# Half of an attention output projection in seven block products, with the operand sums on VectorE

## The chip, the cores and the metric

The kernel runs on one core of a Trainium2 chip. The core has five engines that run side by side, each with its own instruction queue: TensorE (PE, matrix products; its weight loads are listed as PEld), VectorE (DVE), ScalarE (ACT), GpSimd (POOL) and SyncE (SP, which only starts transfers here). The metric is the device time in microseconds of one execution. Two kernels are compared by the median of several executions.

## The reference

A two-layer encoder is run over two sequences, of 512 and 256 tokens, with shared weights. Each layer adds half a gated feed-forward block, a token mixer and another half feed-forward block to the residual stream x. The mixer of the second layer is windowed attention with 16 query heads of 64 channels and 4 key heads. What matters here is its last line:

```python
o = jnp.einsum('bnhgqk,bnkhd->bnqhgd', (p / denom).astype(v.dtype), vband)
return o.reshape(B, T, Hq * d) @ w_o        # (tokens x 1024) times (1024 x 1024)
...
x = x + mix
x = x + 0.5 * swiglu_ffn(rmsnorm(x, norm_g[li, 2]), ffn_w1[li, 1], ffn_w2[li, 1])
```

So each of the 768 tokens' 1024 attention outputs is multiplied with w_o and added to x, then x is normalised and goes into the last feed-forward block, which is called f3.

## The kernel before

**Numbers.** Everything is float32. An operand of a product is split into a high part (rounded to the format that TensorE takes in one pass) and the rest: ScalarE copies the high part, VectorE subtracts (`split`, lines 391 to 393). A product is then three matmuls: high by high, high by low, low by high (`mm3`, lines 385 to 389).

**Memory.** Activations lie in 21 slots of 128 x 1536 floats (`big`, line 91). Raw weights come from memory in tiles of 128 x 1024 (`wr`, four buffers), started on SP's queue, and their split halves go into eight buffers (`w`). A plan lists all weights in the order of their use; `load_next` starts the loads of the next entry when raw buffers are free, and `done` (line 365) frees the buffers of a used weight and stages as many next ones as fit. An accumulating transfer, started on POOL's queue, adds one tile to another in memory (`into`, line 159). A framework under the kernel works out all semaphores and lays down the order of each engine's queue ahead of the run; an instruction can be put ahead of one that stands earlier in the program if its operands are expected earlier.

**Products in blocks.** The feed-forward blocks already multiply 2 x 2 blocks (the two halves of tokens, of the channels summed over, and of the output columns) with seven products instead of eight, at the price of sums of the operands and of the results. `plan_quad` and `quad_steps` (line 209) load and add up the weights for it: p1 to p6 use the raw tiles or sums of them, p7 uses a third sum, s3. `down_last` (line 800) runs the products in the order LAST = p1, p2, p6, p7, p4, p5, p3. FACTOR (line 39) says which activation factor each product takes: b00, b10, b11 are plain blocks, t1 to t4 are sums.

**The attention stage.** `swa` (line 1428) works through 24 units: 4 key heads (groups) times 6 blocks of 128 tokens. `pipeline` (line 1585) interleaves the steps of the units, four steps a unit, and `extra` puts other work at given steps: the query projection, reloading x, splitting attention outputs, and pieces of the output projection. A unit's `finish` (line 1701) writes its outputs into `of[g]`, for the first 21 units by transfers, for the last three by ScalarE and VectorE directly. `of[g]` holds 256 channels of all 768 tokens, so groups 0 and 1 give the first half of the 1024 input channels of w_o, and groups 2 and 3 the second half.

**The output projection** (`out_proj`, line 1514) runs twice. Its first half (groups 0 and 1) is woven into the pipeline from step 66 on. Its second half (groups 2 and 3) follows the pipeline: for each of two column halves and six token blocks, four channel blocks of three matmuls with 512 columns each, then VectorE adds the bank to x (`add_x`, line 846). The outputs of groups 2 and 3 are split by `split_out` (line 1490) in pieces of 512 and 256 columns, those of group 2 from step 83 on, those of group 3 behind the pipeline. In the second column half, each block of x that is complete is normalised by `after_block` (line 590): ScalarE squares and sums it, VectorE scales it. When three blocks are normalised, `turn` (line 470) transposes them on TensorE, ScalarE copies them out and splits them with VectorE into f3's operands (b00 and b10 for the first half of tokens, b01 and b11 for the second). `run_later` starts such deferred steps. f3 opens with `up_first` (line 650): plain products on the first half of tokens, then the products p7 and p3 of a seven-product pair.

Of the kernel before, what the change touches and what calls it, by code (L numbers as in the profile page):

```python
# [9 lines left out]
F32 = mybir.dt.float32  # L10
F32R = mybir.dt.float32r
# [5 lines left out]
P = 128  # L17
D = 1024
DFF = 2816
NC = D // P  # L20
# [14 lines left out]
H = T // 2  # L35
HB = H // P
# [16 lines left out]
LAST = ("p1", "p2", "p6", "p7", "p4", "p5", "p3")  # L53
TAIL = (("b00", "b10"), ("t3", "t2"), ("t4", "t1"), ("b11",))
FACTOR = {"p1": "b00", "p2": "b10", "p3": "b11", "p4": "t4", "p5": "t1", "p6": "t2", "p7": "t3"}
# [3 lines left out]
class Trunk:  # L59
# [149 lines left out]
    def quad_steps(self, key, raws, srcs, order):  # L209
        nc = self.nc  # L210
        flat = lambda t: t.rearrange("p a b -> p (a b)")
        up = len(raws) == 2
        if up:
            a11, a12, a21, a22 = (flat(t[:, h : h + 4, :]) for t in raws for h in (0, 4))
            part = lambda i, k: srcs[i].rearrange("(k p) c -> p k c", p=P)[:, k : k + 4, :]
# [5 lines left out]
        if not up:  # L221
            self.into(a21, a22)
        s3 = []
        for i, src in enumerate(three):
            t = self.wp.tile([P, 512], F32, tag="s3", name=self.name("s3"), bufs=2)
            self.last_load = nc.sync.dma_start(t.rearrange("p (a b) -> p a b", a=src.shape[1]), src)
            self.into(t, a11 if up else a11[:, i * 512 : (i + 1) * 512])
            s3.append(t)
# [21 lines left out]
        add = {"second": lambda: nc.vector.tensor_add(a11, a11, a21), "fourth": lambda: nc.vector.tensor_add(a12, a12, a11)}  # L250
# [3 lines left out]
        if order == OPEN:  # L254
            own.update({"p3": s3[1:], "p7": s3[:1]})
            add = {"second": lambda: self.into(a11, a21)}
            behind, pin = {"p1": "second"}, lambda ins: None
        elif order == DOWN:
            before = {}
            add = {"second": lambda: self.into(a11, a21), "fourth": lambda: self.into(a12, a11)}  # L260
# [938 lines left out]
        quad(("g",), w_in[:, 2 * D : 3 * D], TOK)  # L1199
        quad(("o",), w_o, OUT)  # L1200

    def plan_out(self, tag, w_o):
        for half in range(2):
            for c in range(2):
                for i in range(2):
                    lo = half * 512 + i * 256
                    self.plan((tag, half, c, i), w_o[lo : lo + 256, c * 512 : (c + 1) * 512], (2, 512))

    def plan_swa(self, w_qkv, w_o):
        for tag, c in (("kv", D), ("q0", 0), ("q1", 512)):  # L1210
            self.plan_tok(tag, w_qkv, c)
        self.plan_out("sw_o", w_o)

    def hgrn(self, lb_row, gn_row, next_row):
        nc = self.nc
# [212 lines left out]
    def swa(self, next_row):  # L1428
        nc = self.nc
# [32 lines left out]
        def put_q(half):  # L1462
            def f(s, b, ps):
                gb = SEQS[s][0] // P + b
                if half and gb % 3 == 0:
                    hold.append(self.big([P, 3, 512]))
                t = hold[gb // 3][:, gb % 3] if half else self.xt()[:, :512]
                self.rotate(ps, 512 // HD, b, t)
                for gg in range(2):
                    qtok[(s, b, half * 2 + gg)] = t[:, gg * 256 : (gg + 1) * 256]  # L1470

            hold = []
            return f

        tiles = [None] * NC
        of = {}

        def units(gs):
            def alloc(g):
# [10 lines left out]
        def split_out(g, i, s):  # L1490
            off, n = SEQS[s]
            if s == 0:
                tiles[2 * g + i] = self.big([P, 2, T], F32R)
            hi, lo = (tiles[2 * g + i][:, half, off : off + n] for half in range(2))
            self.split(of[g][:, i, off : off + n], hi, lo)

        q = itertools.chain(self.proj_tok("q0", put_q(0)), self.proj_tok("q1", put_q(1)))
        wo = self.out_proj("sw_o", 0, tiles, None)
        for _ in range(8):
            next(q)  # L1500
        piece = lambda g: lambda: next(g, None)
        extra = [(i * 5 / 4 - 4, piece(q)) for i in range(16)]
        extra += [(18 + 2 * i, piece(q)) for i in range(25)]
        extra.append((46, self.reload_x))
        for n in range(12):
            extra.append(((50, 58, 83)[n // 4] + 2 * (n % 4), lambda n=n: split_out(n // 4, n // 2 % 2, n % 2)))
        extra += [(66 + i * 3 / 2, piece(wo)) for i in range(24)]
        self.pipeline(list(units(range(KV))), extra)
        for n in range(4):
            split_out(3, n // 2, n % 2)  # L1510
        self.drain(wo)
        self.drain(self.out_proj("sw_o", 1, tiles, next_row))

    def out_proj(self, tag, half, act, next_row):
        for c in range(2):
            for b in range(NBLK):
                ps = self.ps()
                sl = slice(b * P, (b + 1) * P)
                for i in range(4):
                    key = (tag, half, c, i // 2)  # L1520
                    wh, wl = self.take(key)
                    t = act[half * 4 + i]
                    self.mm3(ps, (t[:, 0, sl], t[:, 1, sl]), (wh[:, i % 2, :], wl[:, i % 2, :]), i == 0, i == 3)
                    if i == 1:
                        if b == NBLK - 1:
                            self.done(key)
                        yield
                self.add_x(self.x[b][:, c * 512 : (c + 1) * 512], ps, 1.0)
                if b == NBLK - 1:
                    self.done(key)  # L1530
                if half and c:
                    self.after_block(b, next_row)
                    if b in (HB - 1, HB):
                        self.run_later()
                elif not half and b % 2:
                    self.run_later()
                yield

# [293 lines left out]
```

## Time and profile before

| what | us |
|---|---|
| median of 3 executions (2751.13 to 2752.06) | 2751.23 |
| the profiled execution, its own time | 2750.38 |
| its span, from the first to the last instruction | 2748.6 |
| second half of the output projection, in the trace | about 2222 to 2257.4 |

The granted TensorE clock was 0.999 of full speed. The profile comes from one execution. Its page gives the busy time of each engine, the chain of work that ended last (followed back from the last instruction to whatever released it), and the costliest groups of instructions. The trace behind it can be asked for a stretch of time: the busy time of each engine in windows, or the instructions of one engine in order of time. A row of the latter shows start, duration, engine, line of the kernel, operation, output and inputs, and in brackets how long the engine had idled before and what ended the wait. In a row of windows come the stretch and its length, then for PE, PEld, DVE, ACT and POOL the busy time and the number of instructions, then the granted clock, the DMA share and GB/s.

### The profile page before, as it was taken

What the parts mean: (1) busy time and instruction counts of PE and PEld (TensorE: products, weight loads), DVE (VectorE), ACT (ScalarE), POOL (GpSimd) and SP (SyncE); (2) the same over time, 40 slices, a digit from 0 to 9 for tenths busy, and PEclk for the clock granted to TensorE, in tenths of its full rate; (3) what the DMA queues carried; (4) which work ended last, traced back from release to release, by engine and by line L of the source; (5) the groups of instructions that cost most, each with busy time, mean ns of one, the idle gap of its engine ahead of it and who ended that gap; (6) DMA issues with size and microseconds to landing.
All of it is one profiled execution on the core that took longest, in us unless ns stands there. A gap on an engine that the chain in (4) does not pass through costs nothing.

```text
span 2748.6 us, 41245 instructions
## 1 busy us (share of the span) xinstructions
PE 2733.9 (99%) x15059; PEld 2541.0 (92%) x15059; DVE 2164.3 (79%) x3759; ACT 1405.6 (51%) x2665; POOL 500.4 (18%) x566
## 2 busy tenths in 40 slices
PE   9999999999999999999999999999999999999998
PEld 8999999989999889999998999999888889999997
DVE  8788788767877889787878977787847869787877
ACT  6344444634454676444455643444458856444444
POOL 1111121200000111211121121111005621211120
PEclk9999999999999999999999999999999999999999
DMA  6665556741122756556555655555424436555553
GB/s 180 141 143 143 134 136 165 228 140 39 39 59 65 200 131 154 140 142 146 137 129 138 142 142 142 143 139 128 134 75 112 88 76 147 138 145 144 138 127 111
DMA packets 367867, 357.49 MB, mean 130 GB/s; under 512 B 15832, under 2 KB 276400, under 8 KB 367664
## 3 DMA queue, kind: packets, MB, share of 16 engines
q1 hardware_dynamic: 307200, 227.18, 27.8%
q0 software_dynamic: 56160, 114.19, 23.2%
q10 hardware_dynamic: 4304, 13.49, 1.4%
q8 instruction: 118, 1.93, 0.3%
q14 instruction: 85, 0.70, 0.1%
HBM read 228.45 MB, written 15.73 MB: 89 GB/s over the span
## 4 chain that ended last, share of the span: by engine, by line
PE 96%; DVE 2%; ACT 1%; DMA 0%; issue 0%; POOL 0%; ACTq 0%; SPq 0%; DVEq 0%; POOLq 0%
PE ps L678 44%; PE ps L787 17%; PE ps L1003 6%; PE ps L820 6%; PE ps L389 5%; PE ps L388 5%; PE ps L387 5%; PE ps L1066 3%; PE ps L1171 1%; PE ps L484 1%; PE ps L1686 1%; PE ps L1147 1%; PE ps L1698 0%; PE ps L1648 0%; PE ps L1699 0%; PE ps L1649 0%
## 5 line engine op out<-in xcount | busy, mean ns | idle before, releaser
L678 PE MATMUL ps<-big,w 128*128 128x384 f32 x6972 | 1213.2, 334 | 0.0
L678 PEld LDWEIGHTS ps<-big,w 128*128 128x128 f32 x6972 | 1209.5, 188 | 1.4
L243 ACT CAST w<-wr 128x512 fp32r<-128x512 f32 (+1 forms) x615 | 428.6, 706 | 671.8 <-PE ps L678 349.2
L244 DVE TENSOR_TENSOR w<-wr,w 128x512 fp32r<-128x512 f32 (+1 forms) x541 | 437.7, 813 | 141.9 <-ACT w L243 107.7
L787 PE MATMUL ps<-w,big 128*128 128x512 f32 x2016 | 460.9, 390 | 0.0
L787 PEld LDWEIGHTS ps<-w,big 128*128 128x128 f32 x2016 | 376.7, 188 | 80.1 <-ACT big L392 1.5
L850 DVE SCALAR_TENSOR_TENSOR x<-ps,x 128x512 f32<-128x512 f32 x420 | 274.6, 682 | 26.5 <-PE ps L787 13.5
L160 POOL DMA_DIRECT2D s<-wr x135 | 119.6, 935 | 887.4 <-issue 283.6
L160 POOL DMA_DIRECT2D wr<-wr x147 | 129.0, 877 | 796.3 <-DVE big L393 149.9
L393 DVE TENSOR_TENSOR big<-tA,big 128x384 fp32r<-128x384 f32 x308 | 179.2, 593 | 21.1 <-ACT big L392 20.9
L392 ACT CAST big<-tA 128x384 fp32r<-128x384 f32 x308 | 152.6, 514 | 74.1 <-DVE tA L712 29.2
L387 PE MATMUL ps<-big,w 128*128 128x384 f32 x544 | 187.3, 345 | 0.6 <-DVE big L464 0.6
L388 PE MATMUL ps<-big,w 128*128 128x384 f32 x544 | 183.2, 337 | 0.2 <-DVE big L464 0.2
L389 PE MATMUL ps<-big,w 128*128 128x384 f32 x544 | 182.6, 336 | 0.3 <-DVE w L393 0.3
L1003 PE MATMUL ps<-w,big 128*128 128x512 f32 x756 | 178.2, 393 | 0.1
L820 PE MATMUL ps<-w,big 128*128 128x512 f32 x756 | 174.7, 391 | 0.7 <-DVE x L850 0.6
L820 PEld LDWEIGHTS ps<-w,big 128*128 128x128 f32 x756 | 141.1, 188 | 30.8 <-DVE x L850 1.9
L1003 PEld LDWEIGHTS ps<-w,big 128*128 128x128 f32 x756 | 140.3, 188 | 29.0 <-DVE w L393 0.6
L244 POOL TENSOR_TENSOR w<-wr,w 128x512 fp32r<-128x512 f32 x74 | 105.3, 1424 | 122.1 <-ACT w L243 121.4
L393 DVE TENSOR_TENSOR w<-wr,w 128x1024 fp32r<-128x1024 f32 (+1 forms) x74 | 87.8, 1193 | 30.6 <-ACT w L392 28.6
L392 ACT CAST w<-wr 128x1024 fp32r<-128x1024 f32 (+1 forms) x74 | 75.7, 1029 | 69.7 <-PE ps L388 36.0
L706 DVE TENSOR_TENSOR tA<-tA,ps 128x384 f32<-128x384 f32 x80 | 44.0, 550 | 81.4 <-PE ps L678 81.4
(251 smaller groups left out, 3730.0 us busy)
## 6 DMA issues: line engine op xcount, KB each, us to landing
wr<-in_ffn_w_dram SPq DMA_DIRECT2D x254, 512.0 KB, 3.8
s<-wr POOLq DMA_DIRECT2D x135, 256.0 KB, 4.5
s<-in_ffn_w_dram SPq DMA_DIRECT2D x126, 256.0 KB, 3.2
wr<-wr POOLq DMA_DIRECT2D x61, 512.0 KB, 5.5
wr<-wr POOLq DMA_DIRECT2D x86, 256.0 KB, 3.7
wr<-in_hg_w_in_dram SPq DMA_DIRECT2D x32, 512.0 KB, 3.8
spill<-x ACTq DMA_DIRECT2D x12, 512.0 KB, 3.8
kept<-big POOLq DMA_DIRECT2D x8, 768.0 KB, 6.1
```

The costliest lines, as they stand in the source:

```text
L160: self.nc.gpsimd.dma_start(out, src, accum_op=ALU.add)
L243: nc.scalar.copy(h, src)
L244: (eng or nc.vector).tensor_sub(l, src, h.bitcast(F32))
L387: nc.tensor.matmul(out, a[0], b[0], start=first, stop=False)
L388: nc.tensor.matmul(out, a[0], b[1], start=False, stop=False)
L389: nc.tensor.matmul(out, a[1], b[0], start=False, stop=last)
L393: self.last_lo = self.nc.vector.tensor_sub(lo, src, hi.bitcast(F32)).ins
L678: self.nc.tensor.matmul(ps, a[x], b[y], start=first and k == 0 and i == 0, stop=k == 3 and i == 2, skip_group_check=True,)
L787: nc.tensor.matmul(ps, a[x], w[y], start=name == chain and kp == 0 and q == 0, stop=kp == 1 and q == 2, skip_group_check=True,)
L820: nc.tensor.matmul(ps, a[x], w[y], start=name == chain and k == 0 and q == 0, stop=k == 2 and q == 2, skip_group_check=True,)
L850: self.nc.vector.scalar_tensor_tensor(x, ps, c, x, ALU.mult, ALU.add)
L1003: nc.tensor.matmul(ps, x[:, sl], y, start=fresh and k == 0 and q == 0, stop=k == 3 and q == 2, skip_group_check=True,)
```

## The change

The second half of the output projection becomes a 2 x 2 block product with seven products in the order LAST. The token halves are 384 tokens (three blocks), the channel halves are groups 2 and 3, the column halves 512 columns. Its weights are planned as one entry of four raw tiles with `plan_quad`; the third sum of weights takes its two tiles from the activation slots instead of the buffers `s3`, which the attention units use. The splitting of groups 2 and 3 by 128-channel tiles is replaced by seven factors of 384 tokens: b00 and the first subtraction (`lead`) at steps 83 and 86, b10 behind the pipeline, and the others as hooks between the blocks of p1 and p6. The sums t2, t3, t4 are made and split on VectorE and ScalarE in two parts: `early` (256 of the 384 tokens) and `late` (the last 128). `out_quad` adds the results to x: p1 is copied out by ScalarE; p6 and p7 are combined with it on VectorE and also added to a second block of x by accumulating transfers on POOL's queue (`into`); the others are added or subtracted by VectorE. The first token half of x is complete after p4, the second after p3.

```diff
@@ quad_steps
         s3 = []
+        more = self.big([P, 2, 512]) if key[0] == "sw_o" else None
         for i, src in enumerate(three):
-            t = self.wp.tile([P, 512], F32, tag="s3", name=self.name("s3"), bufs=2)
+            t = more[:, i] if more else self.wp.tile([P, 512], F32, tag="s3", name=self.name("s3"), bufs=2)
...
@@ plan_swa (plan_out is taken out)
-        self.plan_out("sw_o", w_o)
+        for c in range(2):
+            for i in range(2):
+                self.plan(("sw_o", 0, c, i), w_o[i * 256 : (i + 1) * 256, c * 512 : (c + 1) * 512], (2, 512))
+        rows = w_o[512:, :].rearrange("(h k p) c -> h p k c", p=P, k=2)
+        srcs = [rows[h][:, :, c * 512 : (c + 1) * 512] for c in range(2) for h in range(2)]
+        self.plan_quad(("sw_o", 1), srcs, (2, 512), LAST)
...
@@ swa
+        whole, early, late = slice(0, H), slice(0, 2 * P), slice(2 * P, H)
+        part = lambda g, half, at=whole: of[g][:, :, half * H + at.start : half * H + at.stop]
+
+        def factor(name, src, at=whole):
+            if name not in facs:
+                facs[name] = self.big([P, 2, 2, H], F32R)
+            self.split(src, *(facs[name][:, :, i, at] for i in range(2)))
+
+        def lead():
+            nc.vector.tensor_sub(part(2, 0), part(2, 0), part(2, 1))
+
+        def mixed(at):
+            add, sub = nc.vector.tensor_add, nc.vector.tensor_sub
+            b11 = part(3, 1, at)
+            for name, op, out, x, y in (
+                ("t2", add, part(2, 0, at), part(2, 0, at), b11),
+                ("t3", sub, part(2, 1, at), part(2, 1, at), b11),
+                ("t4", sub, part(3, 0, at), part(3, 0, at), part(2, 0, at)),
+            ):
+                op(out, x, y)
+                factor(name, out, at)
...
-        for n in range(12):
-            extra.append(((50, 58, 83)[n // 4] + 2 * (n % 4), lambda n=n: split_out(n // 4, n // 2 % 2, n % 2)))
+        for n in range(8):
+            extra.append(((50, 58)[n // 4] + 2 * (n % 4), lambda n=n: split_out(n // 4, n // 2 % 2, n % 2)))
+        extra += [(83, lambda: factor("b00", part(2, 0))), (86, lead)]
         extra += [(66 + i * 3 / 2, piece(wo)) for i in range(24)]
         self.pipeline(list(units(range(KV))), extra)
-        for n in range(4):
-            split_out(3, n // 2, n % 2)
+        factor("b10", part(3, 0))
         self.drain(wo)
-        self.drain(self.out_proj("sw_o", 1, tiles, next_row))
+        hooks = {
+            ("p1", 0): lambda: (factor("t1", part(2, 0)), mixed(early)),
+            ("p1", HB - 1): lambda: mixed(late),
+            ("p6", 0): lambda: factor("b11", part(3, 1)),
+        }
+        for at in self.out_quad("sw_o", facs, next_row):
+            hooks.pop(at, lambda: None)()
...
@@ new
+    def out_quad(self, tag, facs, next_row):
+        nc = self.nc
+        cols = lambda b, c: self.x[b][:, c * 512 : (c + 1) * 512]
+        banks, sums = {}, {}
+        for name in LAST:
+            wh, wl = self.take((tag, 1, name))
+            chain = {"p2": "p1", "p3": "p5"}.get(name, name)
+            h = facs[FACTOR[name]]
+            if name in ("p1", "p7"):
+                sums[name] = self.big([P, HB, 512])
+            for i in range(HB):
+                if name == chain:
+                    banks[(chain, i)] = self.ps()
+                ps = banks[(chain, i)]
+                sl = slice(i * P, (i + 1) * P)
+                for kp in range(2):
+                    a, w = (h[:, kp, 0, sl], h[:, kp, 1, sl]), (wh[:, kp, :], wl[:, kp, :])
+                    for q, (x, y) in enumerate(((0, 0), (0, 1), (1, 0))):
+                        nc.tensor.matmul(
+                            ps,
+                            a[x],
+                            w[y],
...
+                x11, x12, x21, x22 = cols(i, 0), cols(HB + i, 0), cols(i, 1), cols(HB + i, 1)
+                if name == "p1":
+                    nc.scalar.copy(sums["p1"][:, i], ps)
+                elif name == "p6":
+                    nc.vector.tensor_sub(sums["p1"][:, i], sums["p1"][:, i], ps)
+                    self.into(x12, sums["p1"][:, i])
+                elif name == "p7":
+                    nc.vector.tensor_sub(sums["p7"][:, i], ps, sums["p1"][:, i])
+                    nc.vector.tensor_add(x21, x21, sums["p7"][:, i])
+                    self.into(x22, sums["p7"][:, i])
+                elif name == "p5":
+                    nc.vector.tensor_sub(x22, x22, ps)
+                else:
+                    dst = {"p2": x11, "p4": x21, "p3": x12}[name]
+                    nc.vector.tensor_add(dst, ps, dst)
+                if name in ("p4", "p3"):
+                    self.after_block(i if name == "p4" else HB + i, next_row)
+                if (name, i) in (("p5", HB - 1), ("p3", 0)):
+                    self.run_later()
+                yield name, i
+            self.done((tag, 1, name))
```

`out_proj` itself keeps only its first half, and its code for the second half is taken out.

More of the change, by code (lines that the diff above doesn't have):

```diff
@@ L1200, in plan_hgrn @@
         quad(("o",), w_o, OUT)
[L1202 to L1207, printed above, removed]
     def plan_swa(self, w_qkv, w_o):
@@ L1473, in put_q @@
             return f
-        tiles = [None] * NC
-        of = {}
+        tiles = [None] * (NC // 2)
+        of, facs = {}, {}
         def units(gs):
@@ L1495, in split_out @@
             self.split(of[g][:, i, off : off + n], hi, lo)
+        whole, early, late = slice(0, H), slice(0, 2 * P), slice(2 * P, H)
[16 more added lines that the diff above has]
+                factor(name, out, at)
         q = itertools.chain(self.proj_tok("q0", put_q(0)), self.proj_tok("q1", put_q(1)))
-        wo = self.out_proj("sw_o", 0, tiles, None)
+        wo = self.out_proj("sw_o", tiles)
         for _ in range(8):
@@ L1511, in swa @@
         self.drain(wo)
-        self.drain(self.out_proj("sw_o", 1, tiles, next_row))
-    def out_proj(self, tag, half, act, next_row):
+        hooks = {
[27 more added lines that the diff above has]
+                            w[y],
+                            start=name == chain and kp == 0 and q == 0,
+                            stop=kp == 1 and q == 2,
+                            skip_group_check=True,
+                        )
+                x11, x12, x21, x22 = cols(i, 0), cols(HB + i, 0), cols(i, 1), cols(HB + i, 1)
[19 more added lines that the diff above has]
+            self.done((tag, 1, name))
@@ L1515, in out_proj @@
+    def out_proj(self, tag, act):
         for c in range(2):
@@ L1519, in out_proj @@
                 for i in range(4):
-                    key = (tag, half, c, i // 2)
+                    key = (tag, 0, c, i // 2)
                     wh, wl = self.take(key)
-                    t = act[half * 4 + i]
+                    t = act[i]
                     self.mm3(ps, (t[:, 0, sl], t[:, 1, sl]), (wh[:, i % 2, :], wl[:, i % 2, :]), i == 0, i == 3)
@@ L1530, in out_proj @@
                     self.done(key)
[L1531 to L1535, printed above, removed]
+                if b % 2:
                     self.run_later()
```

## The prediction

> **What bounds the kernel now.** I read the profile's page first, then the busy time by windows around the output projection, then the instructions of each engine in order of time.
>
> ```profile
> span 2748.6 us, 41245 instructions
> ...
> PE 2733.9 (99%) x15059; PEld 2541.0 (92%) x15059; DVE 2164.3 (79%) x3759; ACT 1405.6 (51%) x2665; POOL 500.4 (18%) x566
> ...
> PE 96%; DVE 2%; ACT 1%; DMA 0%; issue 0%; POOL 0%; ACTq 0%; SPq 0%; DVEq 0%; POOLq 0%
> ```
>
> The chain that ended last is TensorE at 96%, so a matmul taken away is worth its time wherever TensorE stays fed. Whether it stays fed here is read from the windows (busy time, then instruction counts: PE, PEld, DVE, ACT, POOL). The second half of the projection runs from about 2222 to 2257.4 us.
>
> ```profile
> 2211.50:2224.30 12.80, 12.57 (x63) 9.90 (x62) 10.55 (x17) 6.57 (x11) 1.81 (x4) 1.00 0.20 47
> 2224.30:2257.50 33.20, 33.19 (x159) 27.36 (x158) 15.86 (x25) 15.31 (x28) 4.57 (x6) 1.00 0.39 88
> 2257.50:2273.60 16.10, 15.98 (x101) 15.54 (x100) 15.83 (x22) 15.71 (x30) 4.58 (x5) 1.00 0.53 104
> 2273.60:2300.00 26.40, 26.40 (x154) 26.40 (x153) 26.06 (x45) 19.73 (x37) 5.28 (x6) 1.00 0.71 164
> 1461.50:1507.10 45.60, 45.60 (x214) 37.88 (x213) 41.23 (x65) 24.92 (x43) 6.61 (x8) 1.00 0.50 120
> ```
>
> In the stage itself TensorE is full (33.19 of 33.20) and VectorE works 15.86 us and idles 17.3. Then feed-forward block f3 opens, and there TensorE, VectorE (15.83 of 16.10) and, until 2273.6, ScalarE (15.71) are all full at once; VectorE stays full to 2300. So two resources matter: TensorE's matmuls, which the change saves, and VectorE's slack ahead of f3, which it spends.
>
> **What TensorE saves.** Before: 2 column halves x 6 token blocks x 4 channel blocks x 3 = 144 matmuls of 512 columns. After: 7 products x 3 blocks x 2 x 3 = 126. Their pace is read from VectorE, which idles until each block of 12 is done:
>
> ```profile
> 2224.65 0.69 DVE L848 TENSOR_TENSOR x<-ps,x 128x512 f32<-128x512 f32 x1 [0.39 <-PE ps L389]
> ...
> 2230.09 0.69 DVE L848 TENSOR_TENSOR x<-ps,x 128x512 f32<-128x512 f32 x1 [2.03 <-PE ps L389]
> 2232.81 0.69 DVE L848 TENSOR_TENSOR x<-ps,x 128x512 f32<-128x512 f32 x1 [2.03 <-PE ps L389]
> 2235.53 0.69 DVE L848 TENSOR_TENSOR x<-ps,x 128x512 f32<-128x512 f32 x1 [2.03 <-PE ps L389]
> ```
>
> The last three starts are 2.72 us apart, 0.227 us a matmul; the first row is the stage's first block, so the stage began near 2224.65 - 2.72 = 2221.9. 18 x 0.227 = **4.1 us** saved. The transposes that open f3 stay as they are (24 in both).
>
> [...]
>
> **What VectorE gets.** Prices by pitch (start to start, as it overlaps the ends):
>
> ```profile
> 2214.14 0.69 DVE L393 TENSOR_TENSOR tA<-ps,tA 128x512 fp32r<-128x512 f32 x1
> 2214.75 0.68 DVE L393 TENSOR_TENSOR big<-big,big 128x512 fp32r<-128x512 f32 x1
> ...
> 2219.94 1.23 DVE L393 TENSOR_TENSOR w<-wr,w 128x1024 fp32r<-128x1024 f32 x1 [0.44 <-ACT w L392]
> 2221.08 0.68 DVE L393 TENSOR_TENSOR tA<-ps,tA 128x512 fp32r<-128x512 f32 x1
> ...
> 2223.42 0.84 DVE L1717 TENSOR_TENSOR big<-ps,tA 64x256 f32<-64x256 f32 x2
> ...
> 2225.25 0.75 DVE L393 TENSOR_TENSOR big<-big,big 128x256 fp32r<-128x256 f32 x2
> ...
> 2279.63 3.56 DVE L393 TENSOR_TENSOR big<-big,big 128x768 fp32r<-128x768 f32 x4
> ```
>
> That is 0.61 us for 512 elements, 1.14 for 1024, 0.37 for 256, 0.89 for 768. Row 2223.42 is the last attention unit's output, done at 2224.3; the late quarter of the sums waits for it.
>
> - Ahead of 2224.3: factor b00, the leading subtraction and t1 (0.89 each) take the place of the four splits of group 2 (2 x 0.61 + 2 x 0.37); b10 (0.89) takes that of two splits of group 3 (1.21); the first weight sum (1.14) is new. The window 2211.5 to 2224.3 leaves VectorE 2.25 us idle. Cost taken as nothing, hidden by TensorE's attention matmuls; if that cover is short, what is late joins the next list.
> - Sums and splits (mixed): early 6 x 0.61, late 6 x 0.37, b11 0.89, less the two 256 splits that go: +6.0.
> - Evacuations: p2, p6, p4, p5, p3 three each, p7 six, so 21 instead of 12: +9 x 0.61 = 5.5. p1 is copied by ScalarE, which idles over half of this window.
> - Weights: four plain tiles become seven products. p1, p2, p6, p7 are split where the four were; p4, p5, p3 and the second weight sum are new here: 4 x 1.14 = 4.6.
>
> Together **+16.1 us** on the 15.86 there: 32.0 us of VectorE work in 33.2 - 4.1 = 29.1 us of stage. The overflow is **2.9 us**, and it falls into f3's opening, which has no slack. How little it has:
>
> ```profile
> 2257.43 0.33 PE L387 MATMUL ps<-big,w 128*128 128x384 f32 x1
> ...
> 2260.58 0.33 PE L387 MATMUL ps<-big,w 128*128 128x384 f32 x1
> ...
> 2258.24 1.82 DVE L393 TENSOR_TENSOR big<-big,big 128x768 fp32r<-128x768 f32 x2
> ```
>
> f3's first product starts at 2257.43; its 19th matmul, at 2260.58, is the first to read the second part of operand b10, which VectorE finished at 2258.24 + 1.82 = 2260.06: 0.5 us in hand. So TensorE stalls about there. Overflow 2.9, plus about 1 us in which VectorE must idle for a block of matmuls, less 0.5: **3.4 us**. An independent reading of the same wait is the opening of f2, ahead of which f1's last projection runs in the product order that the change takes over:
>
> ```profile
> 1502.91 4.38 PE L820 MATMUL ps<-w,big 128*128 128x512 f32 x18
> ...
> 1509.23 0.34 PE L387 MATMUL ps<-big,w 128*128 128x384 f32 x1
> 1509.63 0.44 PE L388 MATMUL ps<-big,w 128*128 128x384 f32 x1
> ...
> 1508.62 1.83 DVE L393 TENSOR_TENSOR big<-big,big 128x768 fp32r<-128x768 f32 x2 [0.59 <-ACT big L392]
> ```
>
> There 18 matmuls follow the first block of p3 (1502.91), and b10 comes just in time (0.40 instead of 0.17 us between two starts). The new p3 leaves 12: 6 x 0.227 = 1.4 us less cover, so 1.4 us of stall from latency alone. The ends: 0, since in the stage ahead of f2 (the window from 1461.5) VectorE was at 41.23 of 45.60 and TensorE at 45.60; and 5.7, if VectorE idles here by the same tenth (2.8 of 29.1) on top of the overflow. I take 3.4, nearer to the sum of rows.
>
> **Transfers.** POOL gets nine more accumulating DMAs: three for the weights, six of 256 KB into x12 and x22. First POOL's issues (start, time), then sizes and time from issue to landing:
>
> ```profile
> 2257.36 0.87 POOL L160 DMA_DIRECT2D x<-x  x1 [10.14 <-ACT big L487]
> ...
> 2265.32 0.86 POOL L160 DMA_DIRECT2D x<-x  x1 [1.57 <-ACT big L392]
> ...
> 2277.90 2.68 POOL L160 DMA_DIRECT2D x<-big  x3 [5.20 <-ACT big L572]
> ```
>
> ```profile
> wr<-in_ffn_w_dram SPq DMA_DIRECT2D x9, 512.0 KB, 3.9
> ...
> wr<-wr POOLq DMA_DIRECT2D x4, 256.0 KB, 4.4
> x<-x POOLq DMA_DIRECT2D x3, 256.0 KB, 3.6
> x<-big POOLq DMA_DIRECT2D x3, 256.0 KB, 4.3
> ```
>
> The only wait added on them is p5's subtraction on VectorE, behind the adds into x22. p7's first block ends 60 matmuls on (2235.5) and p5's first 96 on (2243.7). VectorE's two operations, 0.9 of issue and 4.3 of landing give 2242, so it is hidden, by 1.7 us. Behind that subtraction on VectorE stand f3's operand splits. x12 is asked for 72 matmuls, 16 us, after p6: hidden. f3's weights load later:
>
> ```profile
> 2268.81 3.45 PE L678 MATMUL ps<-big,w 128*128 128x384 f32 x19
> ```
>
> The raw buffers come free only as p4, p5 and p3 are split (about 2231 to 2240), but f3's first weights are due at 2253 and the first that needs weight sums 11 us later, as it was before (2257.43 to 2268.81): hidden.
>
> **The rivals.**
>
> *Clean*: VectorE's carried work is f3's later weights, and nothing waits. 2751.2 - 4.1 = 2747.1. For it: f2's opening, full at 90% VectorE. Against it: 32.0 us in 29.1.
>
> *The x22 adds come late* (the slower side). f3's four weight adds share POOL's queue. If they are queued ahead of the x22 adds, these wait until f3's raw weights have landed (p3's split near 2240, two loads of 3.9: 2247), for two issues, a landing of 4.4 for the chained add and their own 0.9 and 4.3: 2258. VectorE then stands 10 us before p5's subtractions with f3's splits behind them, and TensorE about as long less the 0.5 of slack: -4.1 + 9.5 = +5.4, **2756.6 to 2758**. It decides once the first x22 add is issued later than 2239.4. Against it, POOL's queue follows expected readiness, not the program: there each x-from-x add alternates with an x-from-big one, and in the rows above all of the former went 12 us ahead.
>
> [...]
>
> *Lasting lag*: VectorE, full to 2300, cannot recover, and f3's next products stall too: twice the stall, 6.8 - 4.1 = +2.7, 2753.9.
>
> *Attention disturbed*: the four raw tiles load together, and POOL's adds for them wait ahead of its softmax scaling. POOL already waited like this, and TensorE's longest wait in the stretch was 1.1 us:
>
> ```profile
> 2162.47 1.98 POOL L160 DMA_DIRECT2D big<-tA  x2 [4.30 <-DMA big<-tA]
> ```
>
> ```profile
> PE ps L1648 <- ACT tA L1639: 1.3, 2, 1.1
> ```
>
> I price it at 0 to 4.3, take 2: +1.3 with the forecast's stall, 2752.5.
>
> **How the numbers follow.** The profiled execution took 2750.4 us (span 2748.6 and 1.8 around it): 2750.4 - 4.1 + 3.4 = 2749.7. The median of the three runs is 0.8 above it, so **2750.5**. The forecast's own range is 2747.1 to 2752.8 (stall 0 to 5.7). Chances: forecast 0.52, clean 0.18, lasting lag 0.13, attention 0.08, late adds 0.09. The range reaches into lag and attention: 2747.0 to 2755.0. 0.2% is 5.5 us, about what a measurement here can tell from no change; faster than that would need more than the 4.1 that is saved (0.02); slower needs the late adds or a longer lag (0.09); the same, 0.89.
>
> **What would show it.** 126 matmuls of 512 at 0.227 us in the new stage, and its end 4 us earlier: right on the saving. VectorE idle for under 2 us between 2225 and f3's start, and TensorE waiting on VectorE's splits or ScalarE's copies within 5 us of f3's start, 2 to 5 us in all: right on the cost. TensorE never waiting: the clean rival. VectorE waiting for a DMA into x before p5's subtractions: the late adds. A TensorE wait on t2, t3 or t4 inside the stage would be a wait that I cost at nothing.

## The result and the profile after

The changed kernel takes **2766.84 us** (median of 6, 2764.03 to 2768.45) beside 2751.64 for the kernel before (6 runs): ratio 1.0055, 95% interval 1.0042 to 1.0068, so 15.2 us slower. The profiled execution took 2764.96 us, its span is 2763.2 us, and the granted clock was 0.997 (before 0.999).

The page after, the lines that answer to those of before:

```profile
span 2763.2 us, 41282 instructions
...
PE 2736.2 (99%) x15041; PEld 2541.2 (92%) x15041; DVE 2182.4 (79%) x3783; ACT 1411.8 (51%) x2674; POOL 509.2 (18%) x575
...
PE 95%; DVE 2%; DMA 1%; ACT 1%; issue 0%; POOL 0%; ACTq 0%; SPq 0%; POOLq 0%; DVEq 0%
```

TensorE has 18 matmuls less and is busy 2.3 us more, mostly because matmuls behind a stall ran at a lower granted clock (0.71 from 2253.75 to 2270.34). The place is found by landmarks. The stage began at 2221.9 before and begins at 2226.25 now (+4.35), although one and the same attention matmul stands at 2162.91 in both traces. From there to f3's first 384-column matmul it took 35.5 us and takes 44.1 (2226.25 to 2270.34: +8.6). From there to the end of the span it took 491.2 and takes 492.9 (+1.7). These three make up the 14.6 us between the spans.

TensorE's rows in order of time, after:

```profile
2169.70 0.78 PE L1757 MATMUL ps<-ident_r,big 128*128 128x128 f32 x2 [1.07 <-POOL big L1751]
...
2226.25 24.64 PE L1559 MATMUL ps<-w,big 128*128 128x512 f32 x108
2253.75 3.87 PE L1559 MATMUL ps<-w,big 128*128 128x512 f32 x10 [2.86 <-DVE x L1578]
2264.10 2.39 PE L485 MATMUL ps<-ident_r,big 128*128 128x128 f32 x10 [6.48 <-DVE big L446]
...
2271.99 0.44 PE L389 MATMUL ps<-big,w 128*128 128x384 f32 x1 [1.03 <-DVE big L394]
```

p1 to p5 are 108 matmuls without a gap (24.64 / 108 = 0.228 us each, one record for each call). Then p3, which accumulates in the banks of p5, waits 2.86 us until VectorE has subtracted p5's bank from x22 (L1578). Then the transposes of the turn wait 6.48 us for a normalised block (L446). What held VectorE stands in its own rows, and what held those in GpSimd's:

```profile
2247.58 0.68 DVE L1574 TENSOR_TENSOR big<-ps,big 128x512 f32<-128x512 f32 x1
...
2255.05 0.69 DVE L1578 TENSOR_TENSOR x<-x,ps 128x512 f32<-128x512 f32 x1 [1.45 <-DMA x<-big]
2262.50 0.69 DVE L1578 TENSOR_TENSOR x<-x,ps 128x512 f32<-128x512 f32 x1 [6.76 <-DMA x<-big]
```

```profile
2245.61 0.86 POOL L160 DMA_DIRECT2D x<-big  x1 [1.12 <-DVE big L1574]
2247.61 0.85 POOL L160 DMA_DIRECT2D x<-big  x1 [1.14 <-DVE x L1575]
2251.69 0.86 POOL L160 DMA_DIRECT2D s<-wr  x1 [3.23 <-PE ps L1559]
2253.13 0.86 POOL L160 DMA_DIRECT2D s<-wr  x1 [0.58 <-issue]
2255.26 0.86 POOL L160 DMA_DIRECT2D x<-big  x1 [1.28 <-issue]
```

The third sum of p7 was made at 2248.26 (2247.58 + 0.68). Its add into x22 was issued only at 2255.26, behind two sums of f3's weights that waited for their loads, and VectorE got the result at 2262.5, 7 us later. The transfers of this stretch (KB, median us from issue to landing) and the windows (PE, PEld, VectorE, ScalarE, GpSimd, granted clock, DMA share, GB/s):

```profile
wr<-in_ffn_w_dram SPq DMA_DIRECT2D x6, 512.0 KB, 7.1
x<-big POOLq DMA_DIRECT2D x6, 256.0 KB, 7.2
```

```profile
2226.25:2253.75 27.50, 24.64 (x110) 20.12 (x108) 27.31 (x42) 15.59 (x25) 5.88 (x7) 0.99 0.53 119
2253.75:2270.34 16.59, 10.10 (x43) 7.91 (x43) 6.10 (x12) 5.87 (x14) 5.12 (x6) 0.71 0.84 176
...
2255.00:2260.00 5.00, 2.62 (x8) 1.71 (x7) 0.69 (x1) 1.86 (x5) 1.75 (x2) 0.84 1.16 271
```

VectorE is full up to p3's wait (27.31 of 27.50) and nearly idle behind it (6.10 of 16.59), where it waits for transfers. The DMA engines are full there (share 1.16), and the landings that took 3.9 and 4.3 us before take 7.1 and 7.2. The clock is 0.71: p3's first ten matmuls took 3.87 us instead of 2.27. The stage adds up: -4.1 saved, +2.86 and +6.48 waited, some +3.4 of lower clock, together the 8.6. (Of the 3.4, 1.6 are lost at these ten. The rest is lost from 2264.10 on: 24 transposes and 8 matmuls take 6.24 us, and some 4.4 at the paces of the kernel before, 0.11 and 0.227 us.)

In these shorter stretches the clock has two values only, 1.00 and 0.50, and the lower one lasts 3.41 us (2171.28, 2253.20) or 6.83 (2260.03):

```profile
2167.87:2171.28 3.41, 1.74 (x7) 0.69 (x5) 1.12 (x2) 0.89 (x2) 3.41 (x7) 1.00 0.99 149
2171.28:2174.70 3.42, 3.42 (x13) 3.13 (x14) 2.08 (x6) 1.79 (x5) 3.42 (x8) 0.50 0.72 100
...
2249.79:2253.20 3.41, 1.10 (x5) 0.56 (x3) 3.41 (x6) 2.55 (x5) 0.93 (x2) 1.00 1.13 243
2253.20:2256.62 3.42, 2.87 (x7) 2.32 (x8) 1.09 (x2) 3.41 (x8) 1.65 (x2) 0.50 1.13 274
2256.62:2260.03 3.41, 1.00 (x5) 0.48 (x3) 0.00 (x0) 0.24 (x1) 0.89 (x1) 1.00 1.14 264
2260.03:2263.44 3.41, 0.00 (x0) 0.00 (x0) 0.94 (x4) 0.00 (x0) 0.00 (x0) 0.50 0.83 153
2263.44:2266.86 3.42, 2.76 (x12) 2.66 (x13) 3.42 (x7) 0.00 (x0) 2.09 (x3) 0.50 0.06 11
2266.86:2270.27 3.41, 3.40 (x22) 2.48 (x20) 1.05 (x2) 2.70 (x6) 1.04 (x2) 1.00 1.07 182
```

Each halved stretch follows one in which TensorE computed for 1.74 us or less of 3.41.

VectorE's own work came out near the forecast: from the stage's first matmul to f3's it was busy 18.17 us before and 33.41 after, 15.2 more. Before, then after:

```profile
2221.93:2257.43 35.50, 35.48 (x168) 29.25 (x168) 18.17 (x29) 15.84 (x29) 4.50 (x6) 1.00 0.42 96
```

```profile
2226.25:2270.34 44.09, 34.74 (x152) 28.02 (x150) 33.41 (x54) 21.46 (x38) 11.00 (x12) 0.88 0.65 141
```

The 4.35 us ahead of the stage come from the attention. GpSimd there, after:

```profile
2165.28 2.01 POOL L160 DMA_DIRECT2D big<-tA  x2 [5.52 <-ACT big L1735]
2166.60 2.51 POOL L160 DMA_DIRECT2D big<-wr  x2
2168.76 2.47 POOL L1751 TENSOR_SCALAR big<-big,stat 128x256 f32<-128x256 f32 x4
```

Two weight sums of the change (big<-wr) stand between a unit's outputs and the next softmax scaling (L1751), for which TensorE waits 1.07 and once more 0.36 us; in the 3.41 us from 2171.28 on the clock is 0.50.

### The profile page after: what moved, and what is told of

It is laid out like the page before. It is cut to its first block, busy times and chain, and to the rows that moved or that the text cites. A ratio compares the mean times of both kernels' runs of the same rounds, so it can differ in the third digit from the quotient of the medians.

```text
span 2763.2 us, 41282 instructions
## 1 busy us (share of the span) xinstructions
PE 2736.2 (99%) x15041; PEld 2541.2 (92%) x15041; DVE 2182.4 (79%) x3783; ACT 1411.8 (51%) x2674; POOL 509.2 (18%) x575
## 4 chain that ended last, share of the span: by engine, by line
PE 95%; DVE 2%; DMA 1%; ACT 1%; issue 0%; POOL 0%; ACTq 0%; SPq 0%; POOLq 0%; DVEq 0%
PE ps L679 43%; PE ps L788 17%; PE ps L1004 6%; PE ps L821 6%; PE ps L389 5%; PE ps L390 5%; PE ps L388 5%; PE ps L1067 3%; PE ps L485 1%; PE ps L1172 1%; PE ps L1757 1%; PE ps L1148 1%; DVE big L394 0%; DMA big<-tA 0%; PE ps L1720 0%
## 5 line engine op out<-in xcount | busy, mean ns | idle before, releaser
L679 PEld LDWEIGHTS ps<-big,w 128*128 128x128 f32 x6972 | 1209.4, 188 | 1.6 <-ACT tA L696 0.2
L244 ACT CAST w<-wr 128x512 fp32r<-128x512 f32 (+1 forms) x621 | 434.7, 709 | 679.5 <-PE ps L679 346.5
L389 PEld LDWEIGHTS ps<-big,w 128*128 128x128 f32 x544 | 102.4, 188 | 2.4 <-DVE big L394 1.7
```

Of the source, the lines that this page charges most:

```text
L244: nc.scalar.copy(h, src)
L389: nc.tensor.matmul(out, a[0], b[1], start=False, stop=False)
L679: self.nc.tensor.matmul(ps, a[x], b[y], start=first and k == 0 and i == 0, stop=k == 3 and i == 2, skip_group_check=True,)
```

## The experiments

Theories at the start: **A**, the adds onto x12 and x22 as transfers come late; **B**, VectorE has more work than the stage has room for; **C**, the weight loads and sums disturb the attention. Each is a rival of the others for the 15 us. Line numbers shift by some lines between the kernels. Medians in us, each with the kernel before in the same batch (2750.91 to 2751.53):

| run | median (range) | ratio [95%] |
|---|---|---|
| e1_no_adds | 2756.89 (2754.03 to 2759.95) | 1.0020 [1.0010, 1.0029] |
| e2_x_on_vector | 2758.99 (2757.95 to 2759.83) | 1.0027 [1.0017, 1.0037] |
| e3_sums_late | 2762.96 (2762.28 to 2763.34) | 1.0040 [1.0025, 1.0055] |
| e4_both | 2756.91 (2755.29 to 2757.73) | 1.0019 [1.0010, 1.0028] |
| e5_low_on_pool | 2761.37 (2760.15 to 2762.41) | 1.0037 [1.0023, 1.0050] |
| e6_own_banks | 2758.47 (2756.99 to 2760.40) | 1.0027 [1.0017, 1.0037] |
| e7_f3_later | 2756.01 (2754.62 to 2757.53) | 1.0019 [1.0009, 1.0029] |
| e8_low_x12 | 2761.82 (2759.39 to 2761.85) | 1.0036 [1.0023, 1.0049] |
| e9b_sums_moved | 2755.04 (2753.83 to 2759.67) | 1.0014 [1.0005, 1.0023] |
| e9_relief | 2759.14 (2758.87 to 2761.33) | 1.0030 [1.0018, 1.0041] |
| e10_order | 2765.39 (2762.77 to 2766.71) | 1.0049 [1.0036, 1.0062] |
| e11_x22_first | 2762.80 (2762.04 to 2765.54) | 1.0041 [1.0028, 1.0055] |
| e12_floor | 2751.57 (2750.62 to 2753.75) | 1.0001 [0.9992, 1.0010] |

**The adds taken away (e1).**

```diff
-                    self.into(x12, sums["p1"][:, i])
-                    self.into(x22, sums["p7"][:, i])
```

> Leaves out the six accumulating transfers into x12 and x22, so these blocks of x lack the terms of p6 and p7; VectorE's work is unchanged. Theory A (the third add into x22 lands late, p5's subtraction on VectorE waits 6.8 us for it, and TensorE waits 2.9 + 6.5 us behind it, with some 3 us more from the lower clock after it): 11 to 13 us less than the changed kernel, 2754 to 2756. Theory B (the forecast: VectorE's overflow of about 3 us is the main cost): no more than 2 us less, 2765 or above.

10.0 us less than the changed kernel. The 6.48 us wait is gone, VectorE no longer waits for a transfer, and what is left at p3 is VectorE's own queue. TensorE in e1:

```profile
2252.01 4.11 PE L1559 MATMUL ps<-w,big 128*128 128x512 f32 x10 [2.77 <-DVE x L1576]
```

A holds, and beside it B at 2.77 us. Ten matmuls in 4.11 us instead of 2.27 show the clock again (0.60 from 2253 to 2256). Not all of the 10.0 us are the adds' own: the stage up to f3 takes 36.24 us (2224.59 to 2260.83) instead of 44.09, 7.9 less. Another 1.35 us are gained ahead of the stage, where no add runs: the waits on GpSimd are there as before (1.39 and 0.36 us), but in this execution the clock stayed at 1.00 behind them (2165 to 2200).

**The adds on VectorE (e2).**

```diff
-                    self.into(x12, sums["p1"][:, i])
+                    nc.vector.tensor_add(x12, x12, sums["p1"][:, i])
-                    self.into(x22, sums["p7"][:, i])
+                    nc.vector.tensor_add(x22, x22, sums["p7"][:, i])
```

> The six additions into x12 and x22 are done by VectorE instead of by transfers; 6 x 0.61 = 3.7 us more on VectorE. Theory A: as without the adds, plus at most the 3.7: 2754 to 2759. Theory B: VectorE's overflow doubles, so 2 to 4 us more than the changed kernel, 2769 to 2771.

Six adds of 0.61 us are 3.7 us on VectorE, and the wait at p3 grows from 2.8 to 6.4: us for us. So B is a queue on VectorE that TensorE pays in full. All the same 7.9 us less than with transfers.

**The weight sums later (e3).** The s3 loads and three accumulating sums of w_o are issued behind the split of p1's weights.

```diff
+        def thirds():
+            if not up:
+                self.into(a21, a22)
+            for i, src in enumerate(three):
...
+            if out and name == "p1":
+                thirds()
```

> The two loads and three accumulating transfers for the sums of weights are issued behind the split of p1's weights (about 30 us later, in attention) instead of with the raw tiles. Theory C (they and the raw loads hold back the attention's own transfers on POOL's queue, which moves the start of the stage by 4.3 us): TensorE's wait on POOL near 2169 goes and the stage starts near 2222, 3 to 5 us less, 2762 to 2764. Rival: the stage's waits hang on the raw weights' own loads, and the 4 us come back there, 2766 to 2768; or the attention waits just as long at the later place.

3.9 us less. The attention no longer waits for GpSimd, and the stage begins at 2222.42, so C holds. A stays as it was: 3.1 us at p3 and 7.15 at the turn.

**Both (e4): e2 and e3.**

> Both: additions into x on VectorE, and the sums of weights issued later. If A and C hold and add up: 2750 to 2755. If VectorE's overflow then shows as forecast (about 3 us, and up to 3.7 more by the six additions), the upper half of this; if VectorE were no limit, 2747.5.

2756.91, only 2.1 us under e2, though the disturbance cost 3.9 in e3. The profiled executions point to the clock: in e2's, as in e1's, it did not fall in the attention (1.00 from 2150 to 2220), so the disturbance was smaller there. From the landmark in the attention to the stage it took 61.87 us in e2 and 59.70 in e4 (2.2 less), but 63.34 in the changed kernel and 59.58 in e3 (3.8 less). The wait at p3 is 6.4 us again:

```profile
2255.14 2.47 PE L1567 MATMUL ps<-w,big 128*128 128x512 f32 x5 [6.37 <-DVE x L1586]
```

**VectorE's work given to GpSimd (e5, e8).** The low halves of the weights of p4, p5 and p3 and one weight sum on GpSimd; e8 also has the x12 adds as transfers again.

```diff
-            split(name, own[name], nc.gpsimd if spare and name == "p5" else None)
+            split(name, own[name], nc.gpsimd if spare and name == "p5" or out and name in ("p4", "p5", "p3") else None)
```

> As e4_both, with the low halves of the weights of p4, p5 and p3 and the sum of weights ahead of p3 made by GpSimd, so four operations of 1.14 us each leave VectorE. Theory B' (VectorE's backlog at the end of the stage, 9 us in e4_both, is what TensorE waits for: p3 adds into p5's banks and so waits until VectorE has emptied them): the backlog falls by 4.6, the wait of 6.4 us to about 1.8, with less lost to the lower clock behind it: 4.6 to 6.5 us less than e4_both, 2750.5 to 2752.5. Rival D (the wait comes from the order of p5, the transposes and p3, whatever VectorE's load): under 1 us less, 2756 to 2758.

> As e5_low_on_pool, with the three additions into x12 as accumulating transfers again (they are not needed until p3 is done), so 6.4 us of VectorE work less than in e4_both. Theory B': no wait left at p3 or under 1 us, and with it no lower clock: 7 to 9 us less than e4_both, 2748 to 2750, which is the before kernel less some 2 us. If transfers into x collide with f3's weight loads at any place (theory A taken broadly): slower than e5_low_on_pool by 2 us or more.

Both miss: 4.5 and 4.9 us slower than e4, the wait at p3 7.58 and 7.95 us. VectorE has four operations less and is slower in others. GpSimd, then VectorE, in e5:

```profile
2228.42 2.55 POOL L251 TENSOR_TENSOR w<-wr,w 128x1024 fp32r<-128x1024 f32 x1 [13.84 <-ACT w L250]
2234.59 2.40 POOL L251 TENSOR_TENSOR w<-wr,w 128x1024 fp32r<-128x1024 f32 x1 [3.61 <-ACT w L250]
2236.94 2.59 POOL L257 TENSOR_TENSOR wr<-wr,wr 128x1024 f32<-128x1024 f32 x1
```

```profile
2227.43 4.43 DVE L1523 TENSOR_TENSOR big<-big,big 128x512 f32<-128x512 f32 x4
2231.78 2.22 DVE L402 TENSOR_TENSOR big<-big,big 128x512 fp32r<-128x512 f32 x4
...
2234.59 0.68 DVE L1589 TENSOR_TENSOR x<-ps,x 128x512 f32<-128x512 f32 x1
2235.19 4.62 DVE L402 TENSOR_TENSOR big<-big,big 128x256 fp32r<-128x256 f32 x2
```

Four operations on two tiles of `big` take 4.43 us while GpSimd computes (2.23 in e4), and four of the same size behind them 2.22, when it doesn't; two of 256 columns take 4.62 (0.78 in e4). The one that reads a PSUM bank (x<-ps,x) keeps its pace, 0.68 us beside GpSimd's work from 2234.59 on.

**Banks of its own for p3 (e6, on e4).** p5 is added to x12 separately (three more operations), so that p3 need not wait for p5's subtraction.

```diff
-            chain = {"p2": "p1", "p3": "p5"}.get(name, name)
+            chain = {"p2": "p1"}.get(name, name)
```

> As e4_both, with banks of its own for p3, so that p3 need not wait for p5's banks; p5 is then added to x12 by VectorE too, 3 x 0.61 = 1.8 us more on VectorE. If the shared bank alone makes the wait: 5 us less than e4_both, 2752. Theory B' (the backlog counts, and the transposes that stand between p3's matmuls need the same queue's normalised blocks): the wait moves to the transposes, 0 to 2 us more than e4_both, 2757 to 2759.

The wait only moves on, to the turn:

```profile
2256.17 1.99 PE L493 MATMUL ps<-ident_r,big 128*128 128x128 f32 x8 [8.85 <-DVE big L454]
```

So the shared bank is where the queue shows, not its cause.

**f3's splits behind p5 (e7, on e4).**

```diff
-            self.done((tag, 1, name))
+            (self.release if name in ("p7", "p4") else self.done)((tag, 1, name))
```

> As e4_both, with the splits of f3's first two weight tiles held back until p5 is done, so that 2 x 1.14 us of VectorE work stand behind p5's subtractions and not ahead of them; the sum of VectorE's work is the same. Theory B': the wait falls from 6.4 to about 4.1 us, and up to 2.3 us come back when f3's products need the weights: 0 to 3 us less than e4_both, 2754 to 2757. Rival D: unchanged, 2757.

The wait falls from 6.4 to 4.1, as 2.3 us of weight splits leave VectorE's queue ahead of p3. The time falls by 0.9 only: 1.1 us come back as a wait at f3's opening.

**Two weight sums as transfers (e9b, on e7), and the x12 adds too (e9).**

```diff
+            add = {"second": lambda: self.into(a11, a21), "fourth": lambda: self.into(a12, a11)}
+            behind, pin = {"p1": "second", "p2": "fourth"}, lambda ins: None
```

> e7_f3_later with one thing more: the two 128x1024 weight sums of the quad (1.214 and 1.219 us on VectorE in e7, at 2220.9 and 2241.5) are made by accumulating transfers right behind the splits of p1 and p2, as the feed-forward quads do. Nothing is left out. Backlog theory (what TensorE waits at p3's first matmul is VectorE's queue, us for us): the wait of 4.08 us falls by 1.2 to 2.4, to 1.7 to 2.9, f3 opens that much earlier, and the time goes from 2756.0 to 2753.5 to 2755.0. Rival, the clock (what is lost is mainly the granted clock behind the stall, which any stall takes, whatever its length): the wait falls, but the time stays within 1 us of 2756.0. Rival, transfers (two more accumulating 512 KB transfers disturb the attention before the stage): the stage begins later than 2223.1 by more than 1.5 us, and the time is not under 2756.

> e9b_sums_moved with one thing more: the three adds of p6 onto x12 (3 x 0.684 us on VectorE in e7, at 2238.5 to 2240.9) are accumulating transfers again, as in the changed kernel; the adds onto x22 stay on VectorE. Nothing is left out. Backlog theory: 2.05 us less than in e9b at p3's first matmul, so a wait of 0 to 0.9 us, no drop of the granted clock in 2245 to 2260, and 2750.0 to 2752.5 us, level with the kernel before. Rival (accumulating transfers land late): p3's sums onto x12 wait for the x12 transfers, VectorE idles on a DMA between 2250 and 2258, and the time stays at or above that of e9b. If the clock theory holds, the gain is larger than the wait: over 3 us against e9b once no stall is left.

e9b: the wait at p3 falls to 1.76 us, and the clock stays at 1.00 behind it. But the stage begins at 2224.12 instead of 2223.10 in e7 (an attention wait stands at 2155.97 in both), so the attention takes half of the gain back; 1.0 us is left. e9 is a miss: p3 doesn't wait at all, and yet it is 4.1 us slower than e9b. TensorE, then ScalarE, in e9:

```profile
2261.22 2.18 PE L498 MATMUL ps<-ident_r,big 128*128 128x128 f32 x9 [5.44 <-ACT big L501]
```

```profile
2260.07 0.62 ACT L250 CAST w<-s 128x512 fp32r<-128x512 f32 x1 [4.96 <-DMA s<-wr]
2260.59 1.99 ACT L501 ACTIVATE big<-ps,cols 128x384 f32<-128x384 f32 x4
```

With the three x12 transfers of 256 KB added (issued from 2238.46 on, 5.1 us to landing), a sum of f3's weights (s<-wr) was issued at 2254.04 instead of 2252.84 and landed at 2260.00 instead of 2256.44; its split stood ahead of the turn's copies in ScalarE's queue, and those held TensorE. What was taken from VectorE came back as a late transfer on another engine.

**What made the x22 add late (e10, e11, on the changed kernel).** e10 has e7's edit; in e11 GpSimd's order has the third x22 add ahead of the two weight sums:

```diff
+        with self.tc.issue_after(self.last_x22.ins):
+            for pair in self.held_sums:
+                self.into(*pair)
```

> The changed kernel with one thing changed: behind p7 and p4 their weight buffers are given back without staging f3's next pairs there, so f3's loads on SP, its accumulating sums on GpSimd and its splits come only behind p5; all six adds onto x12 and x22 stay transfers, and the weight sums of the attention stay where the change has them. Nothing is left out. Queue and contention theory (the third add onto x22 is issued at 2255.26 behind two weight sums, and takes 7.14 us at a DMA share of 0.84 to 1.1): it is now issued by 2253.5, takes 4.0 to 5.0 us, lands by 2258.5 instead of 2262.4, and the wait of 6.5 us at the turn transposes falls to 1 to 3; the wait of 2.86 at p3's first matmul falls too, by the 2.3 us of weight splits (to 0.5). The time: 2766.8 less 4 to 7, so 2760 to 2763, unless f3 opens on weights that come late (then f3 waits for them, and some of it is given back). Rival (an accumulating transfer of 256 KB takes 7 us by itself when three are in flight): it lands at 2260.5 or later, and the time stays above 2764.

> The changed kernel with one thing changed: in GpSimd's order the third accumulating add onto x22 stands ahead of the two sums of f3's first weight pair (in the changed kernel it stands behind them, although its data, the third p7 sum, is made at 2248.3); the same transfers are issued, and VectorE's order is that of the changed kernel. Nothing is left out. In e10_order the two sums still stood ahead of it, so that run changed only the splits. Queue theory (the add is late because it stood behind two sums that wait for weights): it is issued by 2249.5 instead of 2255.26 and lands by 2255, p5's last subtraction no longer waits 6.8 us for it, the wait at the turn transposes falls from 6.5 us to 0 to 2, and the time from 2766.8 to 2757 to 2761. Rival, contention (the transfer takes 7 us because weight loads, sums and adds share the DMA engines, wherever it stands): issued at 2249.5 it lands at 2256.5 or later, the wait is 3 us or more, and the time stays at 2762 or above. Rival, something else is late next (f3's weight sums, now behind the add): f3 opens at 2268 or later all the same.

In e10 the order on GpSimd stayed, so it doesn't answer the question of the place. It does show the load: the third x22 add is issued 29.0 us into the stage, as in the changed kernel, but with two of f3's loads held back it lands in 5.0 us instead of 7.1 (DMA share 1.01 instead of 1.16 from 2255 to 2260). The wait at the turn is 4.1 instead of 6.5. In the profiled execution the stage is no shorter all the same (44.38 us): 1.11 us are waited ahead of f3's first matmul instead, and 5.8 us of TensorE's work fall into the halved 6.83 us behind the wait (2260.80 to 2267.63), where the changed kernel has 2.8 (2260.03 to 2266.86). The median falls by 1.4 us. In e11 the add is issued 25.4 us after the stage's first matmul instead of 29.0, but it still takes about 7.6 us (DMA share 1.13 from 2250 to 2260). GpSimd and VectorE in e11:

```profile
2253.96 0.86 POOL L175 DMA_DIRECT2D x<-big  x1 [3.06 <-DVE x L1599]
```

```profile
2261.67 0.69 DVE L1596 TENSOR_TENSOR x<-x,ps 128x512 f32<-128x512 f32 x1 [3.43 <-DMA x<-big]
```

The wait at the turn halves (3.4) and the time falls by 4.0 us. So place in the queue and full DMA engines share the blame: e11 mends the one, e10 a part of the other. (This profiled execution was already 2.4 us late before the attention's disturbance; the median is the better measure.)

**Everything away (e12): e7 without the adds**, so part of the result is missing.

> e7_f3_later (weight sums behind p1's split, f3's pairs staged behind p5) without the six adds of the p6 and p7 sums onto x12 and x22, which are left out, so that part of the result is missing: neither VectorE nor a transfer makes them. It takes away all three causes at once. If they are the whole loss, VectorE has 4.1 us less in front of p3 than in e7, where TensorE waited 4.08 us: the wait at p3's first matmul is 0 to 0.3 us, no granted clock under 0.98 between 2240 and 2257, and the time is that of the forecast's clean case, 2747.1, with 1.5 us to either side (2746 to 2748.5; f3 opens at 2253 to 2255). Rival, a fourth cause not yet found (something in the seven products themselves, or in f3's later staging, costs too): no stall is left at p3, and the time is 2750 or more all the same; the trace must then show where.

2751.57: level with the kernel before, not the clean 2747.1. The stage begins at 2221.94 as before, p3 waits 0.49 us, and the clock is 1.00 throughout. TensorE in e12:

```profile
2247.08 2.55 PE L1567 MATMUL ps<-w,big 128*128 128x512 f32 x10 [0.49 <-DVE x L1584]
...
2251.99 2.50 PE L493 MATMUL ps<-ident_r,big 128*128 128x128 f32 x18
2255.61 0.62 PE L396 MATMUL ps<-big,w 128*128 128x384 f32 x2 [1.11 <-ACT big L401]
2256.60 0.44 PE L397 MATMUL ps<-big,w 128*128 128x384 f32 x1 [0.38 <-DVE big L402]
```

So the rival holds: there is a fourth cause. The 18 last transposes run right ahead of f3, and the copies and splits of what they turned (L401, L402) lie bare: 1.11 and 0.38 us. No run changes this order, so that cause is read from the trace alone. In the kernel before, the last transposes ahead of f3 are these:

```profile
2250.16 1.97 PE L484 MATMUL ps<-ident_r,big 128*128 128x128 f32 x16
```

Between their end and f3's first matmul at 2257.43 stand 24 matmuls of the old stage, 5.3 us of cover, which the new order doesn't have. f3 opens at 2255.61 in e12, 1.8 us earlier than before, out of 4.1 saved. The rest of the gain is lost behind that: 0.8 us up to the end of f3's opening and 1.1 in the 480 us after it. The 1.1 has no wait over 0.9 us behind it and is no more than single executions differ by (e12's profiled one is 0.8 us under its median); it stays open.

No version that computes everything beats the kernel before; e9b comes nearest, 3.7 us behind. Even with the six adds for nothing the seven products only draw level.

## Why the prediction was wrong

The forecast was 2750.5 in 2747.0 to 2755.0; 2766.8 was measured. By its own steps:

- **What TensorE saves, 4.1 us: right.** 108 matmuls in 24.64 us.
- **VectorE's overflow of 2.9 us: right in size, wrong in place.** With the adds left out p3 waits 2.77 us (e1). The prediction put the stall at f3's second operand part (b10); it came at p3's first matmul, because p3 accumulates in banks that p5's subtraction must read first. That wait was in no step. The work behind the figure was right too: 15.2 us more on VectorE, where it had 16.1. That wait and overflow agree within 0.2 us is partly luck, since how long p3 waits depends on what stands ahead of p5's subtraction: e7 moved 2.3 us of it.
- **"Transfers: hidden" is the step that failed.** It let VectorE sum p7's blocks as soon as TensorE had made them, and took the 4.3 us of landing of the kernel before. But its own sum had VectorE full: the first x22 add was issued 19.4 us into the stage (2245.61 - 2226.25), where the prediction had about 15 (13.6 of matmuls, then two operations). And f3's loads fill the DMA engines just then (share 1.13 from 2255.26 to 2262.40): 7.2 us of landing (5.0 for the third add with two loads held back, e10). Without these adds the time is 10.0 us less (e1), some 8 of them in the stage.
- **The rival "the x22 adds come late" was right in mechanism**, to its condition: it decides when the first add is issued more than 17.5 us into the stage (2239.4 - 2221.9), and the third one stood behind f3's weight sums. VectorE stood 6.76 us ahead of p5's last subtraction, and TensorE waited 6.48 us behind it. It had a chance of 0.09, on the argument that GpSimd's order follows readiness. The order is laid down ahead of the run, and there the third add, ready at 2248.26, stood behind sums issued at 2251.69 and 2253.13. That its stall of 9.5 us is close to 2.86 + 6.48 = 9.34 is luck: 2.77 us of that are VectorE's own queue and stay when the adds are gone (e1). What its 2756.6 to 2758 lacked is the attention, the clock and f3's opening.
- **"Attention disturbed": right, mis-sized.** Taken at 2, bounded at 4.3; 4.35 by landmarks, 3.9 undone by e3. The prediction treated it as an alternative to the x22 rival, and both came true.
- **The granted clock is the term that was missing.** Some 3.4 us in the stage, and of the attention's 4.35 about 1.4, by e1 and e2, where the clock didn't fall and the landmark and the stage lie 61.99 and 61.87 us apart instead of 63.34. Each wait was priced at its own length.
- **"1.4 us of stall from latency alone" ahead of f3: right**, 1.11 + 0.38 in e12. The forecast counted it as another reading of the overflow; it comes on top.
- **Lasting lag**: f3 to the end is 1.7 us longer, 1.03 of it the wait at its opening. It didn't double.

## What to carry to other kernels

Before you save matmuls with sums, see that the engine that makes the sums has room in that very stage: here 4.1 us of TensorE were bought with 15 us of VectorE, and what went over the brim was paid nearly one for one (3.7 us of work for 3.6 of wait in e2, 2.4 for 2.3 in e9b). Moving the excess to transfers or to GpSimd mostly changed where it waited: landings took 7.2 us instead of 4.3 beside the next block's weights, and VectorE's operations up to 4.62 us instead of 0.78 beside GpSimd's (e5). Time an added transfer by when its producer will really be done and by landings under that load. Rivals that don't exclude each other can come true together, as the late adds and the attention did here, so their prices should be added and not only weighed against each other; and look for the work that used to cover the next block's opening before you reorder it.

## What was not expected of the hardware

- The granted clock behind short stalls. It was halved for 3.41 us behind waits of 1.07 and 0.36 us (attention, after), for 3.41 us behind 2.86 us (after) and 2.77 us (e1), but stayed at 1.00 behind 1.76 us (e9b). The length of a wait doesn't separate these. In the changed kernel the halved stretches begin at 2171.28, 2253.20 and 2260.03, whole multiples of 3.413 us apart, and each follows a stretch of 3.41 us in which TensorE worked for 1.74 us or less. There both attention waits fall into one stretch, which leaves 1.74 us of work, and the next one is halved. In e1 they are longer (1.39 and 0.36 us), but in stretches of 3.41 us counted back from its own halved one at 2251.99 they fall into two, with 2.00 and 2.85 us of work, and the clock stays:

```profile
2166.65:2170.07 3.42, 2.00 (x9) 1.17 (x7) 1.03 (x3) 1.56 (x6) 3.42 (x6) 1.00 0.82 109
2170.07:2173.48 3.41, 2.85 (x16) 2.30 (x17) 2.02 (x7) 1.52 (x5) 3.41 (x8) 1.00 0.84 141
```

  The work in a stretch doesn't separate all of them either: in e3 the clock was halved behind a stretch with 1.17 us of work (2252.31 to 2255.72) and not behind those with 1.58 and 1.66 (2245.49 to 2252.31); in the 1.74 us above, over half of the time were transposes. What sets the clock was not shown.
- VectorE operations on two SBUF tiles beside GpSimd's work: 4.62 us where e4 has 0.78, and 4.43 where it has 2.23 (e5).
- Accumulating transfers of 256 KB landed in 4.3 us at a DMA share of 0.86 (before, 2277.9 to 2285.0), in 5.0 at 1.01 (e10, 2255 to 2260), in 7.1 at 1.13 (after, 2255.26 to 2262.40) and in 7.6 at 1.13 (e11, 2255 to 2260): at the earlier place in the queue (e11) no sooner than at the later one.
